# Weight sections prepared in an overlapped order in a two-layer hybrid attention and retention kernel

## The chip, the cores and the metric

The kernel runs on one core of a Trainium2 chip. The metric is the device time of one execution in microseconds (us), from the kernel's start to its end on that core; lower is better. Beside it stands one execution that was recorded by the hardware profiler, from which every row below comes.

## What is computed

The input is a sequence of 2048 tokens with 1024 features. Two layers follow each other, and each adds to the stream what a group of heads makes of it: eight heads of chunked softmax attention with a learned bias by distance (64 features each) and four heads of retention with rotary phases (128 features each), both gated. A last normalization ends it.

```python
def hybrid_layer(x, norm_gain, w_in, w_out, rel_bias, cos, sin):
    hn = rms_norm(x, norm_gain)
    proj = hn @ w_in
    aq, ak, av, ag, rq, rk, rv, rg = split(proj)          # 8 sections of 512 columns
    ya = chunked_rel_attention(aq, ak, av, rel_bias)      # own chunk of 64 and 8 before it
    yr = chunkwise_retention(rq, rk, rv, cos, sin)        # decay per head, RMS norm per head
    y = concatenate([ya * silu(ag), yr * silu(rg)])
    return x + y @ w_out
```

The time goes into the products with `w_in` (1024 x 4096) and `w_out` (1024 x 1024) of each layer, in near-fp32 accuracy.

## The kernel before

**Number format.** Each fp32 matrix is split into two f16 halves, hi and lo, and a product is three matmuls (hi·hi, hi·lo, lo·hi). For that, a section of weights is scaled first by a power of two that is found from its sum of squares. That is the preparation that the change touches.

**Tiling.** A layer runs over four head groups `s` (two attention heads and one retention head each), and each group over four token blocks `n` of 512 tokens. A group uses eight sections of 128 columns of `w_in`: four (`TSEC`, line 289) give q, k and the retention's q and k in transposed form, four (`VSEC`, line 290) the values and gates. For each (layer, s, n) the program runs `dense_T` (matmul in line 753), then `dense_V` (matmul in line 772). Each has 12 rounds of eight matmuls of 128x512, which are the bulk of TensorE's work.

**Rounds.** `run` (line 1174) goes over the rounds of a dense pass. In each round it starts what was deferred with `later`, makes one step of the attention of the block before (`attention`, line 798), and pulls steps of background work. An attention block has eight units (a, hx), three rounds each: scores `S` on TensorE, bias and maximum on VectorE (line 824), exponential and the hi copy on ScalarE (827, 829), the lo half on GpSimd (830), a transposing DMA `pT` on SyncE (832), and two units later the product `o` with the values on TensorE (840 to 842). The output is scaled on VectorE (846 to 852). Retention's steps (`r`, `sh`, `rss`, `yr`) lie between.

**Background work.** `push(gen, steps)` hands a generator over with a number of steps; a step runs until the generator's next `yield`. In each round, `run` pulls the steps that are still to do divided by a number of rounds that are left (`thirds`), rounded up. So the number of steps, the number of `yield`s in the generator and `thirds` decide in which round which instruction is written. Where `thirds` is larger than the number of rounds of a pass, the work runs on into the next pass.

**Order.** TensorE, VectorE, ScalarE and GpSimd run their instructions in the order in which the program writes them. SyncE, which issues the DMAs, is ordered by the scheduler from estimated times, apart from those that are put in turn by hand.

**Preparation of the next group's weights.** `prep_T` (line 385) prepares the four transposed sections and is pushed with 25 steps when block n = 1 starts (in the first group of layer 0: n = 3, with 18 thirds). `prep_V` (line 417) prepares the four others and is pushed with 23 steps before `dense_V` of block n = 3; it runs over that pass's 12 rounds and on into `dense_T` of the next group. One section passes through these steps:

- load: 512 KB into one of three buffers of the pool `w4` (line 297)
- square: ScalarE squares the section and adds up (312), VectorE rounds the sum to bf16 (319, `mb`)
- scale: TensorE adds over the partitions by a one-column matmul with ones (326, `ms`) into one of four small PSUM buffers that attention uses too; VectorE makes a power of two of it (328 and 143 to 147)
- split: ScalarE writes the hi half (333), one step later VectorE the lo half (336)
- units: after certain sections a few small products of scales (`T_units`, `V_units`, lines 344 and 400)

In `prep_V` the last two sections share one scale: line 456 adds the two sums, and one scale follows. The path for layer 1's first group (`halves`, `prep_V_next`) and the preparation of `w_out` (`prep_O`, `prep_Omax`) are of their own.

There are six preparations by `prep_T` and six by `prep_V`, three in each layer.

Of the kernel before, what the change touches and what calls it, by code (L numbers as in the profile page):

```python
# [13 lines left out]
ALU = mybir.AluOpType  # L14
# [13 lines left out]
def hybrid_trunk(ctx: ExitStack, tc: tile.TileContext, x, pos, gain, gcol, w_in, w_out, rel, fgain,  # L28
# [8 lines left out]
    act, dve, pool, pe, sp = nc.scalar, nc.vector, nc.gpsimd, nc.tensor, nc.sync  # L37
# [100 lines left out]
    def norm_scale(sq, nm, ig=None, k=14):  # L138

        e = b2.tile([P, 1], I32, tag="p2e", name=f"e{nm}")  # L140
        s = b2.tile([P, 1], I32, tag="p2s", name=f"s{nm}", bufs=8)
        i = b2.tile([P, 1], I32, tag="p2i", name=f"i{nm}", bufs=12)
        dve.tensor_scalar(e, sq.bitcast(I32), 24, 23, op0=ALU.logical_shift_right, op1=ALU.logical_shift_left)
        dve.tensor_scalar(s, e, -1.0, float((190 + k) << 23), op0=ALU.mult, op1=ALU.add)
        dve.tensor_scalar(i, e, float((64 - k) << 23), None, op0=ALU.add)
        if ig is not None:
            dve.tensor_tensor(i.bitcast(F32), i.bitcast(F32), ig, op=ALU.mult)
        return s.bitcast(F32), i.bitcast(F32)

    gains = {}  # L150
# [166 lines left out]
    def lowp(m1, nm):  # L317
        mb = b2.tile([P, 1], BF16, tag="mb", name=f"mb{nm}", bufs=4)
        dve.tensor_copy(mb, m1)
        return mb  # L320

    def allsum(mb, nm, lo=2.0 ** -60, ps=None):

        if ps is None:
            ps = psR.tile([P, 512], F32, tag="small", name=f"ms{nm}")
        pe.matmul(ps[:, 0:1], ones.to_broadcast([P, P]), mb, start=True, stop=True)
        m2 = b2.tile([P, 1], F32, tag="m2", name=f"m2{nm}")
        dve.tensor_scalar(m2, ps[:, 0:1], lo, None, op0=ALU.max)
        return m2
# [54 lines left out]

    def prep_T(l, s, g, halves=False, w=None):
        w = w or Sections(l, s, g, halves)
        w.load(0)
        yield
        for j in range(4):
            if j < 3:  # L390
                w.load(j + 1)
            yield
            w.square(j)
            yield
            yield
            yield
            w.scale(j)
            yield from w.split(j)
# [18 lines left out]
    def prep_V(l, s, g):  # L417
        nm = f"V{l}_{s}"
        g.vh = b3.tile([P, KT, 512], F16, tag="wh", name=f"wh{nm}")
        g.vl = b3.tile([P, KT, 512], F16, tag="wl", name=f"wl{nm}")  # L420
        c0 = s * P
        sts = []

        def ld(j):
            o = VSEC[j] * 512 + c0
            sts.append(load_sec(w_in[l, :, o:o + P], f"{nm}{j}"))

        def sq(j):
            return sumsq(sts[j], f"{nm}{j}", g.vh[:, :, j * P:(j + 1) * P])

        def cv(j, s_):
            return convert(sts[j], g.vh[:, :, j * P:(j + 1) * P], g.vl[:, :, j * P:(j + 1) * P], s_)

        def rest(k):
            for _ in range(k):
                yield

        ld(0)
        ld(1)
        yield  # L440
        iv = [None] * 3
        m1 = [None] * 2
        for j in range(2):
            yield
            m1[j] = lowp(sq(j), f"{nm}{j}")
            yield from rest(3)
            m = allsum(m1[j], f"{nm}{j}")
            sv, iv[j] = norm_scale(m, f"{nm}{j}", gains[l].i)
            yield from cv(j, sv)
            ld(2 + j)  # L450
        yield from rest(1)
        m2 = sq(2)
        yield
        yield from rest(1)
        m3 = sq(3)
        dve.tensor_tensor(m2, m2, m3, op=ALU.add)
        m2 = lowp(m2, f"{nm}2")
        yield
        yield from rest(2)
        m = allsum(m2, f"{nm}2")  # L460
        sv, iv[2] = norm_scale(m, f"{nm}2", gains[l].i)
        for _ in V_units(l, s, g, iv, nm):
            pass
        yield from cv(2, sv)
        yield from cv(3, sv)
        g.vdone = 4
# [683 lines left out]
    def push(gen, steps):  # L1150
        bg.append([gen, steps])
# [17 lines left out]
    def grp(l, s):  # L1169
        if (l, s) not in groups:  # L1170
            groups[l, s] = Grp()
        return groups[l, s]
# [220 lines left out]
    for l in range(DEPTH):  # L1393
        gO = [Grp(), Grp()]
        go = Grp()
        for s in range(NSW):
            g = grp(l, s)
            for n in range(NS):
                first = (l, s, n) == (0, 0, 0)
                if not first:  # L1400
                    st = St()
                    states[l, s, n] = st
                    dT = dense_T(l, s, n, g, st)
                else:
                    st = st0
                if n == 0 and not first:
                    bs, bt = bias_scratch(l, s), bias_tiles(l, s, g)
                    later(3, lambda bs=bs: next(bs))
                    for k in (7, 11, 17, 21):
                        later(k, lambda bt=bt: next(bt))  # L1410
                if (l, s) == (0, 0) and 0 < n < NS - 1:
                    if n == 1:
                        push(t1, TAB_STEPS - 7)
                    pairs = [xs0[0], w4.tile([P, D], F32, tag="w4", name="rows8") if n == 1 else xs0[1]]
                    pairs = [(w_[:, 0:D], w_[:, D:2 * D]) for w_ in (r_.bitcast(F16) for r_ in pairs)]
                    push(norms_from_input(range(4 * n + 4, 4 * n + 8), late[0:4] if n == 1 else None, pairs,
                                          tables(n + 1, [xs0[n + 1][:, i * 256:(i + 1) * 256] for i in range(4)])), 21)
                if (l, s, n) == (0, 1, 1):
                    for l_ in range(1, DEPTH):
                        gr = gain_scale(l_)  # L1420
                        later(2, lambda gr=gr: next(gr))
                        later(10, lambda gr=gr: next(gr))
                        later(18, lambda gr=gr: next(gr))
                if n == (NS - 1 if (l, s) == (0, 0) else 1):
                    if s + 1 < NSW:
                        push(prep_T(l, s + 1, grp(l, s + 1)), 25)
                    else:
                        push(prep_O(l, 0, gO[0], go), 9)
                if n == NS - 1 and s == 1 and l + 1 < DEPTH:
                    gain_load(l + 1)  # L1430
                if n == 2 and s == 2:
                    push(prep_Omax(l, go), 21)
                last = n == NS - 1 and s == NSW - 1
                if last:
                    us = []
                    push(wout_first(l, go, us), 9)
                if not first:
                    run(dT, att, 12 if last else 10 if n == 0 else 18 if (l, s, n) == (0, 0, NS - 1) else 22 if (l, s) == (0, 0) else 24)
                if n == NS - 1:
                    if s + 1 < NSW:  # L1440
                        push(prep_V(l, s + 1, grp(l, s + 1)), 23)
                    else:
                        push(with_turn(prep_O(l, 1, gO[1], go), us), 12)
                run(dense_V(l, s, n, g, st), att, 24 if n == NS - 1 and s < NSW - 1 else 12)
                if first:
                    sp_order.__exit__(None, None, None)
                    ring["free"] = True
                if att[0] is not None:
                    drain(att[0])
                att = [attention(l, s, n, g, st, states.get((l, s, n - 1)))]  # L1450
        pull(1000)
        if l + 1 == DEPTH:
            ring["fg"] = b3.tile([P, D], F32, tag="wh", name="fg")
            sp.dma_start(ring["fg"], fgain.to_broadcast([P, D]))
        wT = Sections(l + 1, 0, grp(l + 1, 0), True) if l + 1 < DEPTH else None
        wo = wout(l, go, gO, us, wT)

        def rounds_of(k):
            run((next(wo) for _ in range(k)), att, k)

        rounds_of(30)
        if l + 1 < DEPTH:
            push(prep_T(l + 1, 0, grp(l + 1, 0), True, wT), 21)
            rounds_of(36)
            pull(1000)
            pV = prep_V_next(l + 1, grp(l + 1, 0))
            next(pV)
            rounds_of(18)
            next(pV)
            rounds_of(6 * NT - 90)  # L1470
            push(pV, 13)
        else:
            rounds_of(6 * NT - 36)
        run(wo, att, 15)
# [60 lines left out]
```

## Time and profile before

| | us |
| --- | --- |
| runs of the kernel | 2062.57, 2067.20, 2067.78 |
| median | 2067.2 |
| the profiled execution | 2061.84 |
| its span, from the first to the last instruction | 2060.0 |

| engine | short name in rows | busy |
| --- | --- | --- |
| TensorE | PE | 97% |
| TensorE's weight loads | PEld | 51% |
| VectorE | DVE | 60% |
| ScalarE | ACT | 55% |
| GpSimd | POOL | 33% |

The granted TensorE clock is 0.996 of full speed over the span.

How to read rows: a timeline row has the start in us from the span's start, the duration, engine, line and operation, what is written and from which tiles it is read (with shape and type), and in brackets the idle time of the engine before it and what ended it. A row of waits has the instruction that waited, what it waited for, then the total in us, the number of times and the longest. A row of windows has the stretch, its length, the busy time of PE, PEld, DVE, ACT and POOL with the number of instructions, the granted clock, the share of the DMA engines and GB/s. SPq is SyncE's DMA queue. Matmuls are pipelined, so a matmul's duration is longer than the distance between two starts, and that distance is the pace.

### The profile page before, as it was taken

What the parts mean: (1) busy time and instruction counts of PE and PEld (TensorE: products, weight loads), DVE (VectorE), ACT (ScalarE), POOL (GpSimd) and SP (SyncE); (2) the same over time, 40 slices, a digit from 0 to 9 for tenths busy, and PEclk for the clock granted to TensorE, in tenths of its full rate; (3) what the DMA queues carried; (4) which work ended last, traced back from release to release, by engine and by line L of the source; (5) the groups of instructions that cost most, each with busy time, mean ns of one, the idle gap of its engine ahead of it and who ended that gap; (6) DMA issues with size and microseconds to landing.
All of it is one profiled execution on the core that took longest, in us unless ns stands there. A gap on an engine that the chain in (4) does not pass through costs nothing. (4 is left out here: it accounts for less than half of the span.)

```text
span 2060.0 us, 39310 instructions
## 1 busy us (share of the span) xinstructions
PE 1997.9 (97%) x14014; PEld 1049.6 (51%) x14014; DVE 1231.2 (60%) x3817; ACT 1137.7 (55%) x2530; POOL 687.9 (33%) x701
## 2 busy tenths in 40 slices
PE   6988999999999999999999999999999999999998
PEld 4444555555555555554444555555555555555443
DVE  6776656556556655666653556555655565567643
ACT  6566665556565654655443546554656565455432
POOL 0244343444344433430003343433344334333100
PEclk9999999999999999999999999999999999999999
DMA  8778664547584764799865546554756775658964
GB/s 230 169 156 177 156 146 112 112 111 166 113 187 111 166 135 101 164 206 262 233 174 120 126 103 149 120 127 103 155 115 145 163 151 126 131 116 188 228 203 135
DMA packets 645700, 313.62 MB, mean 152 GB/s; under 512 B 459232, under 2 KB 602080, under 8 KB 645504
## 3 DMA queue, kind: packets, MB, share of 16 engines
q1 hardware_dynamic: 645504, 311.12, 66.1%
q8 instruction: 109, 1.79, 0.4%
q14 instruction: 87, 0.71, 0.1%
HBM read 123.26 MB, written 41.98 MB: 80 GB/s over the span
## 5 line engine op out<-in xcount | busy, mean ns | idle before, releaser
L830 POOL TENSOR_TENSOR pq<-sc,pq 128x640 f16<-128x640 f32 (+4 forms) x256 | 319.7, 1249 | 861.0 <-ACT pq L829 451.5
L827 ACT ACTIVATE sc<-sc,mq,cT 128x640 f32<-128x640 f32 (+4 forms) x256 | 218.4, 853 | 615.7 <-DVE rl L846 298.3
L772 PE MATMUL dV<-whV,hTh 128*128 128x512 f16 x1024 | 353.3, 381 | 6.9 <-DVE gt L790 6.4
L772 PE MATMUL dV<-whV,hTl 128*128 128x512 f16 x1024 | 352.5, 380 | 0.0
L772 PE MATMUL dV<-wlV,hTh 128*128 128x512 f16 x1024 | 352.5, 380 | 0.0
L753 PE MATMUL dT<-hTh,whT 128*128 128x512 f16 x1008 | 347.0, 379 | 1.3 <-DMA hTh<-xa 1.1
L753 PE MATMUL dT<-hTl,whT 128*128 128x512 f16 x1008 | 347.1, 379 | 0.0
L753 PE MATMUL dT<-hTh,wlT 128*128 128x512 f16 x1008 | 347.1, 379 | 0.0
L772 PEld LDWEIGHTS <-hTh 128*128 128x128 f16 x2048 | 196.5, 98 | 224.0 <-DVE gt L790 9.0
L753 PEld LDWEIGHTS <-whT 128*128 128x128 f16 x2016 | 192.3, 98 | 210.6 <-issue 4.5
L824 DVE CUSTOM_DVE_ANT_0 sc<-S,bias 128x640 f32<-128x640 f32 (+4 forms) x256 | 188.1, 735 | 86.2 <-PE S L821 84.6
L1127 PE MATMUL dO<-whO,yly 128*128 128x512 f16 x512 | 194.7, 380 | 1.4 <-DMA yly<-hTl 1.4
L1127 PE MATMUL dO<-wlO,yhy 128*128 128x512 f16 x512 | 194.8, 380 | 0.0
L1127 PE MATMUL dO<-whO,yhy 128*128 128x512 f16 x512 | 194.7, 380 | 0.0
L829 ACT ACTIVATE pq<-sc 128x640 f16<-128x640 f32 (+4 forms) x256 | 171.5, 670 | 8.1
L1127 PEld LDWEIGHTS <-yhy 128*128 128x128 f16 x1024 | 100.0, 98 | 115.1 <-issue 1.4
L772 PEld LDWEIGHTS <-hTl 128*128 128x128 f16 x1024 | 99.2, 98 | 110.8 <-issue 1.9
L753 PEld LDWEIGHTS <-wlT 128*128 128x128 f16 x1008 | 97.3, 98 | 111.5 <-issue 4.0
L820 PE MATMUL S<-k,q 128*128 128x128 f16 (+3 forms) x592 | 142.0, 266 | 0.0
L840 PE MATMUL o<-v,pT 128*128 128x65 f16 x1120 | 129.4, 193 | 6.0 <-DMA pT<-pq 6.0
L841 PE MATMUL o<-v,pT 128*128 128x64 f16 x1120 | 129.8, 195 | 0.0
L821 PE MATMUL S<-k,q 128*128 128x128 f16 (+3 forms) x592 | 129.3, 266 | 0.0
(352 smaller groups left out, 3464.1 us busy)
## 6 DMA issues: line engine op xcount, KB each, us to landing
q<-qq SPq DMA_DIRECT2D x128, 128.0 KB, 2.4
yyy<-y_d SPq DMA_DIRECT2D x32, 512.0 KB, 4.6
stT<-in_w_in_dram SPq DMA_DIRECT2D x27, 512.0 KB, 4.9
stV<-in_w_in_dram SPq DMA_DIRECT2D x26, 512.0 KB, 4.8
k<-kk SPq DMA_DIRECT2D x128, 64.0 KB, 2.0
swp<-rot SPq DMA_DIRECT2D x64, 128.0 KB, 3.0
tabc<-tab SPq DMA_DIRECT2D x32, 256.0 KB, 2.9
tabs<-tab SPq DMA_DIRECT2D x32, 256.0 KB, 3.1
```

Source lines behind the costliest of these rows:

```text
L753: pe.matmul(ps, w_[:, j, kt, :], h_[:, kt, :], start=(m == 0), stop=(m == 23))
L772: pe.matmul(ps, h_[:, kt, a * P:(a + 1) * P], w_[:, kt, :], start=(m == 0), stop=(m == 23))
L820: pe.matmul(o, st.q[:, hx, 0, cs], k_, start=True, stop=False)
L821: pe.matmul(o, st.q[:, hx, 1, cs], k_, start=False, stop=True)
L824: dve.tensor_tensor_reduce(out=v, in0=S[:, 0:w], in1=g.bias[hx][:, 640 - w:640], scale=1.0, scalar=-3.0e38, op0=ALU.add, op1=ALU.max, accu ...
L827: act.activation(v, v, AF.Exp, bias=m[:, 0:1], scale=g.c[:, 0:1])
L829: act.activation(pq[:, 0:w], v, AF.Copy)
L830: pool.tensor_tensor(pq[:, w:2 * w], v, pq[:, 0:w], op=ALU.subtract)
L840: pe.matmul(o[:, 0:65], u.p[:, b, :], v_[:, 0:65], start=(b == 0), stop=False)
L841: pe.matmul(o[:, 0:64], u.p[:, b, :], v_[:, 65:129], start=False, stop=False)
L1127: pe.matmul(ps, h_[:, kt, :], w_[:, kt, :], start=(m == 0), stop=(m == 23))
```

## The change

In both generators the order of sections is changed from one after the other to an overlapped one: sections 0 and 1 are loaded in the first step; the square of a section is written, then one step later the scale and the split of the section before it; sections 2 and 3 are loaded after the squares 0 and 2. `prep_T` ends with one more step and the scale and split of section 3; `prep_V` with two steps, the joint scale of sections 2 and 3, the units and both splits. The number of yields falls, and with it the steps pushed: 25 to 19 for `prep_T`, 23 to 20 for `prep_V`. The instructions themselves are the same in kind and number on every engine. The path with `halves` keeps the old order.

```diff
@@ -384,6 +384,23 @@
 
     def prep_T(l, s, g, halves=False, w=None):
         w = w or Sections(l, s, g, halves)
+        if not halves:
+            w.load(0)
+            w.load(1)
+            for j in range(4):
+                for _ in range((2, 2, 0, 1)[j]):
+                    yield
+                w.square(j)
+                if j in (0, 2):
+                    w.load((j + 4) // 2)
+                yield
+                if j:
+                    w.scale(j - 1)
+                    yield from w.split(j - 1)
+            yield
+            w.scale(3)
+            yield from w.split(3)
+            return
         w.load(0)
         yield
         for j in range(4):
@@ -431,34 +448,32 @@
         def cv(j, s_):
             return convert(sts[j], g.vh[:, :, j * P:(j + 1) * P], g.vl[:, :, j * P:(j + 1) * P], s_)
 
-        def rest(k):
-            for _ in range(k):
-                yield
+        def scale(j):
+            sv, iv[j] = norm_scale(allsum(m[j], f"{nm}{j}"), f"{nm}{j}", gains[l].i)
+            return sv
 
         ld(0)
         ld(1)
-        yield
-        iv = [None] * 3
-        m1 = [None] * 2
-        for j in range(2):
-            yield
-            m1[j] = lowp(sq(j), f"{nm}{j}")
-            yield from rest(3)
-            m = allsum(m1[j], f"{nm}{j}")
-            sv, iv[j] = norm_scale(m, f"{nm}{j}", gains[l].i)
-            yield from cv(j, sv)
-            ld(2 + j)
-        yield from rest(1)
-        m2 = sq(2)
-        yield
-        yield from rest(1)
-        m3 = sq(3)
-        dve.tensor_tensor(m2, m2, m3, op=ALU.add)
-        m2 = lowp(m2, f"{nm}2")
-        yield
-        yield from rest(2)
-        m = allsum(m2, f"{nm}2")
-        sv, iv[2] = norm_scale(m, f"{nm}2", gains[l].i)
+        iv, m = [None] * 3, [None] * 3
+        for j in range(4):
+            for _ in range((2, 2, 0, 1)[j]):
+                yield
+            m1 = sq(j)
+            if j < 2:
+                m[j] = lowp(m1, f"{nm}{j}")
+            elif j == 2:
+                m2 = m1
+            else:
+                dve.tensor_tensor(m2, m2, m1, op=ALU.add)
+                m[2] = lowp(m2, f"{nm}2")
+            if j in (0, 2):
+                ld((j + 4) // 2)
+            yield
+            if 0 < j < 3:
+                yield from cv(j - 1, scale(j - 1))
+        yield
+        yield
+        sv = scale(2)
         for _ in V_units(l, s, g, iv, nm):
             pass
         yield from cv(2, sv)
@@ -1423,7 +1438,7 @@
                         later(18, lambda gr=gr: next(gr))
                 if n == (NS - 1 if (l, s) == (0, 0) else 1):
                     if s + 1 < NSW:
-                        push(prep_T(l, s + 1, grp(l, s + 1)), 25)
+                        push(prep_T(l, s + 1, grp(l, s + 1)), 19)
                     else:
                         push(prep_O(l, 0, gO[0], go), 9)
                 if n == NS - 1 and s == 1 and l + 1 < DEPTH:
@@ -1438,7 +1453,7 @@
                     run(dT, att, 12 if last else 10 if n == 0 else 18 if (l, s, n) == (0, 0, NS - 1) else 22 if (l, s) == (0, 0) else 24)
                 if n == NS - 1:
                     if s + 1 < NSW:
-                        push(prep_V(l, s + 1, grp(l, s + 1)), 23)
+                        push(prep_V(l, s + 1, grp(l, s + 1)), 20)
                     else:
                         push(with_turn(prep_O(l, 1, gO[1], go), us), 12)
                 run(dense_V(l, s, n, g, st), att, 24 if n == NS - 1 and s < NSW - 1 else 12)
```

Written out by rounds of the token block's 24, with the first push (layer 0, n = 3) apart, steady state: before, the T squares are written at rounds 2, 8, 14, 20 and their scales at 5, 11, 17, 23; after, the squares at 3, 6, 9, 13 and the scales at 7, 10, 14, 17. For V (V0 to V11 are the rounds of `dense_V` of block 3, d0 on those of the next group's `dense_T`), the last square moves from d4 to d1, the joint scale with the units from d7 to d4, and the last lo half from d10 to d7.

## The prediction

> **What bounds the kernel now.** I read the page first, then the windows by stage, then what PE waits for, and last the timelines round one preparation of the second kind.
>
> ```profile
> span 2060.0 us, 39310 instructions
> PE 1997.9 (97%) x14014; PEld 1049.6 (51%) x14014; DVE 1231.2 (60%) x3817; ACT 1137.7 (55%) x2530; POOL 687.9 (33%) x701
> ...
> 195.00:290.00 95.00, 89.07 (x690) 48.10 (x691) 54.42 (x198) 61.11 (x136) 34.73 (x33) 1.00 0.70 161
> 290.00:860.00 570.00, 568.48 (x4232) 304.44 (x4231) 337.64 (x1150) 325.06 (x765) 223.10 (x222) 1.00 0.60 132
> ...
> 1070.00:1860.00 790.00, 787.54 (x5731) 417.80 (x5730) 452.69 (x1509) 441.83 (x1043) 301.98 (x301) 1.00 0.59 130
> ```
>
> PE is the bound: 97% of the span, and 568.48 of 570 us and 787.54 of 790 us in the two long windows (PE is the first busy time of a row, DVE the third, ACT the fourth). Those windows hold five of the six preparations; there the change has 570 − 568.48 + 790 − 787.54 = 4.0 us of idle PE to take away, whatever waits it removes on other engines. What idle time it could remove lies in the first preparation, 195 to 290 us, with 95 − 89.07 = 5.9 us. The waits of PE in that window:
>
> ```profile
> PE msT L326 <- DVE mbT L319: 2.3, 3, 1.3
> PE msV L326 <- DVE ya L852: 2.1, 2, 1.5
> PE msV L326 <- DVE mbV L319: 1.3, 1, 1.3
> PE dT L753 <- DMA hTh<-xa: 1.1, 1, 1.1
> ...
> 230.47 0.16 PE L326 MATMUL msT<-mbT,ones 128*128 128x1 bf16 x1 [0.56 <-DVE mbT L319]
> ```
>
> Six waits (3 + 2 + 1) at the one-column matmul that sums the squares over the partitions: 2.3 + 2.1 + 1.3 = 5.7 us. These are the waits that a longer distance between square and scale can remove.
>
> **The pace of PE.** Matmuls of 512 columns, after a long wait and after a shorter one:
>
> ```profile
> 931.96 0.20 PE L840 MATMUL o<-v,pT 128*128 128x65 f16 x1 [2.45 <-DMA pT<-pq]
> ...
> 934.26 0.63 PE L1127 MATMUL dO<-wlO,yhy 128*128 128x512 f16 x1
> 934.69 0.63 PE L1127 MATMUL dO<-whO,yly 128*128 128x512 f16 x1
> ...
> 270.03 0.16 PE L326 MATMUL msV<-mbV,ones 128*128 128x1 bf16 x1 [1.51 <-DVE ya L852]
> 270.05 0.38 PE L753 MATMUL dT<-hTl,whT 128*128 128x512 f16 x1
> 270.27 0.38 PE L753 MATMUL dT<-hTh,whT 128*128 128x512 f16 x1
> ```
>
> They start 0.216 us apart at full pace (270.05 to 270.27), so a round of eight takes 1.7 us. After a wait of 2.45 us they start 0.43 us apart, for eight of them: 8 × (0.43 − 0.216) = 1.7 us more. After one of 1.51 us nothing is added. So a new stall below 1.5 us costs its own length, and one above 2.45 us 1.7 more. The Trainium skill ("TensorE: Matmul & The Clock Gate", Part 1: The HAM clock gate) says that the half rate comes after an idle window of about 3.4 us. By that rule stalls of 2.4 us in the slower rival below would cost nothing beside their length; the row of 2.45 us here disagrees, and the row decides.
>
> **The loads.** Two at once changes next to nothing: the buffers' loads land in 4.9 us, and few instructions wait for them.
>
> ```profile
>   DVE mbT L319: 43.1, 23
> ...
>   ACT whT L312: 1.2, 1
> DMA to landing us min/median/max: 3.2/4.9/7.5
> ...
> 452.04 0.38 SPq L297 DMA_DIRECT2D stV<-in_w_in_dram  x1
> ```
>
> That is the view of the transposed sections' load buffer: what waited for its readers (a scale on PE or DVE's rounding, 43.1 us of idle engines off the path), one square of 1.2 us, and the landing times; the last row is a load of SP's timeline, whose section is squared at 471.33 (below), 19 us later. In the built program, SP's queue takes the first three loads of a group as their buffers come free already before the change; only the fourth moves, by one transposed attention block. I cost it at 0; cover is the time that a section lies in its buffer before its square. Without that cover a square would be up to 1.2 us late, the one wait of the view.
>
> **First preparation (fourth token block of the first group), −3.0 us.** Counted in rounds by the step budget, the four T scales stand 1, 1, 3 and 2 rounds behind their squares before (two steps a round), and 4, 4, 5 and 2 after (one step a round at the end of the pass, another square between); the first V scale 3 before and 4 after. The longest of these waits is 1.3 us, under the 1.7 of one round, so two of the msT waits go and the one on `mbV`; the third msT wait is the fourth scale's, at 230.47, and with 2 rounds it keeps its 0.56. The two waits on `ya` are for an older attention unit's result, which must leave a PSUM buffer first; the scales that have them stand three rounds behind their squares before and after, so I leave them standing. (2.3 − 0.6) + 1.3 = 3.0 us. Bounds: −5.7 (all six) and 0 (each is replaced by the next item in DVE's order).
>
> **T preparations of the other five groups: 0.** Nineteen steps instead of 25 over the same 24 rounds: the squares come up to seven rounds earlier, the finished weights four, and each scale stands four rounds behind its square instead of three. They run under attention that is short (second token block); the windows above show PE with 0.3% idle there. If cover failed, the price is one lo half on DVE, 1.28 us (the row at 481.90 below), per section.
>
> **V preparations: the new cost.** They run from the V pass of a group's last token block through ten rounds of the next group's first pass, beside long attention. Twenty steps in place of 23 bring the last square, the joint scale with the units of V, and the last two halves three rounds (one attention unit, 475.24 − 468.55 = 6.7 us with its waits) forward. The order on DVE and ACT is the program's, so this block goes in front of another unit. One of the six windows, before, on DVE and then ACT:
>
> ```profile
> 468.55 0.82 DVE L824 CUSTOM_DVE_ANT_0 sc<-S,bias 128x640 f32<-128x640 f32 x1 [0.31 <-PE S L821]
> ...
> 472.49 0.47 DVE L456 TENSOR_TENSOR m1V<-m1V,m1V 128x1 f32<-128x1 f32 x1 [2.85 <-ACT whV L312]
> ...
> 475.24 0.82 DVE L824 CUSTOM_DVE_ANT_0 sc<-S,bias 128x640 f32<-128x640 f32 x1 [0.71 <-PE S L821]
> ...
> 476.24 0.15 DVE L328 TENSOR_SCALAR m2V<-msV 128x1 f32<-128x1 f32 x1
> ...
> 479.91 0.16 DVE L410 TENSOR_TENSOR gqkV<-gqkV 128x1 f32<-128x1 f32 x1 [2.89 <-ACT reV L407]
> ...
> 481.90 1.28 DVE L336 SCALAR_TENSOR_TENSOR wlV<-stV,sV,whV 128x1024 f16<-128x1024 f32 x1 [0.21 <-ACT whV L333]
> ...
> 484.70 0.82 DVE L824 CUSTOM_DVE_ANT_0 sc<-S,bias 128x640 f32<-128x640 f32 x1
> ```
> ```profile
> 471.33 1.04 ACT L312 ACTIVATE whV<-stV 128x1024 f16<-128x1024 f32 x1
> ...
> 476.42 0.92 ACT L827 ACTIVATE sc<-sc,mq,cT 128x640 f32<-128x640 f32 x1 [3.28 <-DVE m2V L328]
> 477.37 0.74 ACT L829 ACTIVATE pq<-sc 128x640 f16<-128x640 f32 x1
> 478.01 0.19 ACT L193 ACTIVATE urvV<-dcs 128x1 f32<-128x1 f32 x1
> ...
> 479.58 0.29 ACT L407 ACTIVATE reV<-reV,gqkV 128x1 f32<-128x1 f32 x1
> ...
> 480.74 1.13 ACT L333 ACTIVATE whV<-stV,sV 128x1024 f16<-128x1024 f32 x1
> ```
>
> Here `sc` at 468.55 is the second unit (0,1) of attention, 475.24 the third (1,0), 484.70 the fourth (1,1). Between the third and the fourth stands the block from `m2V` at 476.24 to the first lo half, which ends at 481.90 + 1.28 = 483.18: 6.9 us, in which DVE waits 2.89 for ACT's unit operations, which wait for the third unit's exponential and copy. The third unit has only the last square ahead of it and a gap of 2.85.
>
> After, that block stands between 468.55 and 475.24. Its start is the end of the second unit's `sc` and `mq`, about 1.1 us after 468.55, and the second unit itself comes about 1.5 us late, because DVE now waits for the last square (1.04 us on ACT) ahead of it: 471.1. The row distances of the block then give: scale till 471.9; ACT's exponential and copy 1.7, so units on ACT from 472.8 to 474.7 (478.01 to 479.87 before); DVE's six small operations and the older unit's output to 476.2; hi half 1.13 beside them to 476.7, lo half to 478.0; rope's `kk` and retention's state, which stand there anyway, about 1 us; `sc` at 479.0. That is 479.0 − 475.24 = 3.7 us late. The lower bound takes the block as 6.9 less the 0.9 us of attention's own work in it, less the two gaps of 2.85 and 0.71 that it fills: 2.4 us. I take 3.5, near the step by step value, which follows the order.
>
> Who waits for it: ACT's exponential, POOL's lo, SP's transpose, then PE.
>
> ```profile
> 478.24 1.39 POOL L830 TENSOR_TENSOR pq<-sc,pq 128x640 f16<-128x640 f32 x1 [5.29 <-issue]
> ...
> 478.54 0.58 SPq L637 DMA_DIRECT2D tabc<-tab  x1
> ...
> 480.19 1.78 SPq L832 DMA_TRANSPOSE pT<-pq  x1
> ...
> 485.00 2.38 SPq L297 DMA_DIRECT2D stT<-in_w_in_dram  x2
> ...
> DMA to landing us min/median/max: 4.0/5.6/5.6
> ...
> 487.11 0.19 PE L840 MATMUL o<-v,pT 128*128 128x65 f16 x1
> ...
> PE o L840 <- DMA pT<-pq: 0.3, 1, 0.3
> ```
>
> Before: issued at 480.19, landed 4.0 to 5.6 us later (the three transposes of this stretch), at 484.2 to 485.8; PE takes it at 487.11. In hand: 1.3 to 2.9 us. The issue stood 0.56 us behind POOL's end (478.24 + 1.39 = 479.63) in SP's queue, behind table and bias loads; a later transpose need not. So it is 3.5 − 0.5 = 3.0 late at the queue, and PE waits between 3.0 − 2.9 = 0.1 and 3.0 − 1.3 = 1.7 us. On SP one load of 512 KB (one of the two at 485.00) moves ahead of the third unit's transpose in the built program; it takes DMA time there, which speaks for the upper half. I take 0.9 a window, six windows: +5.4 us; bounds 0 and, with the full 3.7 and a backlog at 5.6 us, 2.4 each, +14.4. The fourth unit, the late one today (PE waits 0.3 us for its transpose in the window 1470 to 1500 us, the last row), is relieved in return; little is to be had there.
>
> **The sum.** 2061.8 (profiled execution: span 2060.0 and 1.8 around it) − 3.0 + 0 + 5.4 = 2064.2. The median of the runs shown, 2067.2, lies 5.4 above that execution; so 2069.6, against 2067.2.
>
> **Rivals.** Faster: in the V windows landings are at the quick end (4.0 us), so slack holds, and all six waits of the first preparation go; 5.7 us less, and the fourth unit's relief is worth up to 0.3 in each of six windows, 1.8: 2067.2 − 7.5 = 2059.7. For it: DVE is 60% busy and has time to catch up. Against it: DVE's in-order waits, not its load, make the delay.
>
> Slower: the moved block makes PE wait for the third unit's transpose by the upper bound, 2.4 us in each of six windows, and each then pays 1.7 at the lower clock: 6 × 4.1 − 3.0 = 21.6, 2088.8; without the clock 6 × 2.4 − 3.0 = 11.4, 2078.6, which I give as this rival's time. It decides from a stall of (6.2 + 3.0) / 6 = 1.5 us a window on. For it: four of the values in the chain are estimates from in-order rows that tend to add up, and the load moved ahead. Against it: in the trace PE hardly waits for transposes in these windows.
>
> The change doesn't do what it says: preparation is hidden but for the first one, whose waits turn into waits for the next item on DVE: 2067.2.
>
> **How the numbers follow.** Forecast (about even, 2069.6) 0.38; no effect at all 0.06; faster 0.21; slower 0.35. A change of under 0.3%, 6.2 us, can't be told from none here. Faster by more than that: 0.20, the rival but for its weaker cases. Slower by more: 0.37, the slower rival and the upper edge of the forecast. Within: 0.43. Low end of the range 2059, the faster rival's time with 0.7 us to spare; high end 2084, between the slower rival without and with the clock. The forecast's own range is 2063 to 2075.
>
> **What would show it.** In the first preparation: PE idle of 195 to 290 us falls from 5.9 to about 3, and the list of waits there loses two of msT and the `mbV` one. In the V windows: the `m2V` block stands between the second and third `sc`, the third `sc` starts some 3.5 us later against PE's matmuls, and the line of PE's `o` waiting for pT gains up to six entries of about 0.9. If those entries are missing, the slack is larger than I read; if they exceed 2 us with matmuls 0.43 apart behind them, the slower rival holds. It would be wrong at the root if the T windows, costed at 0, showed waits of PE at dense matmuls for `wlT`, or if the long windows together gained more than the 4.0 us that they have to give.

## The result

| | median us | runs |
| --- | --- | --- |
| before | 2064.0 | 10, from 2061.5 to 2067.8 |
| after | 2070.1 | 10, from 2067.1 to 2074.0 |

The ratio is 1.0027, with an interval of 1.0018 to 1.0036: the change costs 6.0 us by the medians, and between 3.7 and 7.4 by the interval. That it costs something is clear of the noise. The predicted 2069.6 lies 0.5 us off, but that is partly luck: the forecast was a move of +2.4 from the 2067.2 of three runs, and ten runs put the start at 2064.0. A start that was 3.2 too high and a move that was 3.6 too small nearly cancel. What has to be explained is +6.0 where +2.4 was worked out.

The page of the changed kernel, and then the windows that the prediction used (length, then busy time of PE, PEld, DVE, ACT and POOL, the granted clock, the share of the DMA engines, GB/s):

```profile
span 2068.9 us, 39344 instructions
PE 1999.9 (97%) x14014; PEld 1048.5 (51%) x14014; DVE 1226.2 (59%) x3817; ACT 1138.4 (55%) x2530; POOL 684.2 (33%) x701
```
```profile
195.00:290.00 95.00, 89.20 (x692) 47.71 (x691) 59.47 (x208) 61.24 (x139) 36.01 (x34) 1.00 0.75 164
290.00:860.00 570.00, 565.14 (x4195) 301.78 (x4194) 333.60 (x1138) 321.65 (x756) 220.72 (x219) 1.00 0.58 130
...
1070.00:1860.00 790.00, 783.14 (x5683) 414.82 (x5682) 442.22 (x1499) 437.96 (x1032) 294.55 (x296) 1.00 0.58 129
```

In the first preparation PE is idle for 95 − 89.2 = 5.8 us, as before (5.9). In the two long windows its idle time grew from 1.5 to 4.9 and from 2.5 to 6.9, together by 7.7 us. So the gain did not come, and the cost is in the two long windows, which hold the five preparations in steady state. What PE waited for in the three windows, in this order, of the changed kernel (total, times, longest):

```profile
PE o L855 <- DMA pT<-pq: 3.5, 3, 1.7
PE r L889 <- DVE dT L897: 1.5, 2, 1.4
PE o L855 <- DVE ya L867: 0.8, 1, 0.8
...
PE o L855 <- DMA pT<-pq: 2.9, 2, 2.0
...
PE o L855 <- DMA pT<-pq: 4.7, 3, 2.2
```

The first three rows are the first preparation. All six waits at `ms` are gone from it (5.7 us before), and 3.5 + 1.5 + 0.8 = 5.8 us of other waits stand in their place. The other two rows are the five V windows (the stretches of the V preparations) that lie in the long windows: one wait each, for the third unit's transpose, 7.6 us in all, where before there was one of 0.3, for a fourth unit's.

The V window that the prediction followed, on DVE after the change:

```profile
466.15 0.47 DVE L467 TENSOR_TENSOR m1V<-m1V,m1V 128x1 f32<-128x1 f32 x1 [2.85 <-ACT whV L312]
...
469.11 0.82 DVE L839 CUSTOM_DVE_ANT_0 sc<-S,bias 128x640 f32<-128x640 f32 x1
...
470.10 0.15 DVE L328 TENSOR_SCALAR m2V<-msV 128x1 f32<-128x1 f32 x1
...
473.77 0.16 DVE L427 TENSOR_TENSOR gqkV<-gqkV 128x1 f32<-128x1 f32 x1 [2.89 <-ACT reV L424]
...
475.76 1.28 DVE L336 SCALAR_TENSOR_TENSOR wlV<-stV,sV,whV 128x1024 f16<-128x1024 f32 x1 [0.42 <-ACT whV L333]
...
477.76 0.82 DVE L839 CUSTOM_DVE_ANT_0 sc<-S,bias 128x640 f32<-128x640 f32 x1
...
483.61 0.82 DVE L839 CUSTOM_DVE_ANT_0 sc<-S,bias 128x640 f32<-128x640 f32 x1
```

The second unit's `sc` at 469.11, then the block from `m2V` to the lo half, then the third unit's `sc` at 477.76. SP's queue, the landing time of the one transpose issued at 482.18, and PE:

```profile
478.19 0.38 SPq L297 DMA_DIRECT2D stT<-in_w_in_dram  x1
...
481.05 0.43 SPq L600 DMA_DIRECT2D bias<-toep  x1
482.18 2.25 SPq L847 DMA_TRANSPOSE pT<-pq  x1
```
```profile
DMA to landing us min/median/max: 6.3/6.3/6.3
```
```profile
488.50 0.20 PE L855 MATMUL o<-v,pT 128*128 128x65 f16 x1 [1.96 <-DMA pT<-pq]
...
489.68 1.03 PE L787 MATMUL dV<-whV,hTl 128*128 128x512 f16 x4
```

The transpose lands at 482.18 + 6.3 = 488.48, and PE starts at 488.50, 1.96 us after it was free. Before, the same transpose had a landing time of its own of 5.6 us:

```profile
DMA to landing us min/median/max: 5.6/5.6/5.6
```

Two things are later, then: the issue, and the landing after it. Counted back from when PE was ready (487.11 before, 488.50 − 1.96 = 486.54 after), `sc` starts 11.87 us ahead before and 8.78 after, 3.1 later; the issue 6.92 ahead before and 4.36 after, 2.6 later; the landing takes 0.7 more. 2.6 + 0.7 less the slack of 1.3 (487.11 − 485.8) is the wait of 2.0. Ahead of the transpose stands, 4 us earlier, a load of 512 KB that before stood behind it.

### The profile page after: what moved, and what is told of

Its sections match the earlier page's. It is cut to its first block, busy times and chain, and to the rows that moved or that the text cites. A ratio compares the mean times of both kernels' runs of the same rounds, so it can differ in the third digit from the quotient of the medians.

```text
span 2068.9 us, 39344 instructions
## 1 busy us (share of the span) xinstructions
PE 1999.9 (97%) x14014; PEld 1048.5 (51%) x14014; DVE 1226.2 (59%) x3817; ACT 1138.4 (55%) x2530; POOL 684.2 (33%) x701
## 5 line engine op out<-in xcount | busy, mean ns | idle before, releaser
L855 PEld LDWEIGHTS <-pT 128*128 128x128 f16 x1120 | 105.5, 97 | 55.5 <-DMA pT<-pq 25.4
```

What stands on the lines that cost most here:

```text
L855: pe.matmul(o[:, 0:65], u.p[:, b, :], v_[:, 0:65], start=(b == 0), stop=False)
```

## The experiments

Theories on record: *block* (VectorE's order makes the third unit late), *load* (the 512 KB ahead of the transpose do), *T* (the denser work on the transposed sections), *square* (the last square ahead of the second unit), and, from the second set on, *two-part* (block and load are each within the slack, their sum is not).

| run | median us | ratio to before, interval |
| --- | --- | --- |
| T sections alone | 2061.1 | 0.9990 (0.998 to 1.000) |
| V sections alone | 2070.5 | 1.0034 (1.0022 to 1.0046) |
| block three steps later | 2067.8 | 1.0028 (1.0018 to 1.0037) |
| T loads held | 2062.0 | 0.9994 (0.9985 to 1.0003) |
| T and w_out loads held | 2061.2 | 0.9986 (0.9976 to 0.9996) |
| before, loads held | 2061.1 | 0.9987 (0.9978 to 0.9995) |
| T sections alone, loads held | 2061.8 | 0.9988 (0.9979 to 0.9996) |
| block one step later | 2070.4 | 1.0030 (1.0019 to 1.0041) |
| before, loads held, copy added | 2062.2 | 0.9999 (0.9991 to 1.0008) |
| after, loads held, copy added | 2070.9 | 1.0045 (1.0030 to 1.0060) |
| block three steps later, loads held | 2066.4 | 1.0021 (1.0012 to 1.0030) |

The ratios are to runs of the kernel before that were taken beside each set; their medians are 2062.3 (the first four runs of the table), 2063.7 (the next four) and 2062.8 (the last three).

### One generator at a time

The new `prep_T` with the old `prep_V` and 23 steps for it, and the other way round with 25 steps for `prep_T`. One line of the first, against the changed kernel:

```diff
...
-                        push(prep_V(l, s + 1, grp(l, s + 1)), 20)
+                        push(prep_V(l, s + 1, grp(l, s + 1)), 23)
...
```

> The new order for the transposed sections alone (19 steps); the V sections as before (23 steps). Block theory (the cost of the change is the V block of joint scale, units and lo half in front of the third attention unit): no wait of PE for pT at the third unit in the windows after 290 us, and two of the three msT waits of the first preparation gone; 1 to 5 us less than before. T theory (the denser T squares and splits cost): half or more of the 6 us of the change, so 3 us or more above before.

> The new order for the V sections alone (20 steps); the transposed sections as before (25 steps). Block theory: the five waits of the later windows for the third unit's pT stay as in the changed kernel (1.0 to 2.3 us each, 8 to 10 us in all with the slow matmuls behind one of them), so 6 to 11 us above before. T theory: within 2 us of before.

Measured: T alone 1.3 us less with an interval that touches no change, V alone 8 us more than before's 2062.3 (7.0 by the ratio). The whole cost is in the V sections. T alone, waits of PE in the first preparation:

```profile
PE msV L326 <- DVE ya L869: 3.4, 3, 1.5
PE dT L770 <- DMA hTh<-xa: 1.0, 1, 1.0
PE o L857 <- DVE ya L869: 0.8, 1, 0.8
PE r L891 <- DVE dT L899: 0.4, 1, 0.4
```

The three waits of `msT` on `mbT` are gone, as expected or better; but the three V scales wait for `ya` now, 3.4 us where `ya` and `mbV` had 2.1 + 1.3 = 3.4 before, and `o` waits for `ya` too. So the gain of that part is about 1 us (5.7 against 3.4 + 0.8 + 0.4). V alone, the third unit's waits in the two long windows:

```profile
PE o L838 <- DMA pT<-pq: 4.0, 2, 2.0
...
PE o L838 <- DMA pT<-pq: 2.5, 3, 1.7
```

Five waits of 6.5 us: those of the changed kernel, without anything of T. The load is ahead of the third unit's transpose here too, by 4.2 us:

```profile
484.03 0.53 SPq L297 DMA_DIRECT2D stT<-in_w_in_dram  x1
...
488.27 2.10 SPq L830 DMA_TRANSPOSE pT<-pq  x1
```

With T alone it stands behind that transpose, as before (two loads at 485.68, the transpose at 480.77). So the load moves with the V sections, though it belongs to the transposed ones.

### The block back in its old place

```diff
+        yield
+        yield
+        yield
         yield
         yield
         sv = scale(2)
```

> The changed kernel with three more steps ahead of the joint scale of the V sections, and nothing else: scale, units and splits of the last two sections fall where they fell before, the last square stays where the change puts it. Block theory: the waits for the third unit's pT go, the gain of the first preparation stays; 2 to 6 us less than before, 8 to 12 less than the changed kernel. Square theory (the last square ahead of the second unit is what makes attention late): the waits stay, 6 us above before.

In the order of the program, DVE's work round the third unit is that of the kernel before, and SP takes the load after the transpose again. The waits at the third unit are gone; the one wait for pT that is left in the long windows, 1.1 us at 703.8, is the fourth unit's. Yet the time hardly falls: 1.0028. Neither theory had both. The first preparation shows a new wait:

```profile
PE dV L790 <- ACT whV L333: 2.4, 1, 2.4
PE o L858 <- DMA pT<-pq: 2.1, 1, 2.1
```

There the first dense V tile of the next group comes before the last hi half of its weights. In the first preparation the change had moved the block by two rounds only, so by the built order three more steps put that half one round later than before. On ACT it now stands behind the exponential of the fourth unit (275.83) and behind a step on the `bias` table that waits 1.97 us for GpSimd:

```profile
279.49 0.83 ACT L609 ACTIVATE bias<-bias,ciT 128x640 f32<-128x640 f32 x1 [1.97 <-POOL bias L608]
...
280.42 1.13 ACT L333 ACTIVATE whV<-stV,sV 128x1024 f16<-128x1024 f32 x1
```

The square theory falls by the waits: the last square stood ahead of the second unit, and the third unit's waits were gone. It falls by the time as well in a run further down, where the square and the block both stay in the changed place and the loads are held (0.9986). The profiled execution here (2064.8 us) was 2.9 us faster than the median of its runs; what the others lose beyond it stays open.

With one more step in place of three:

> The changed kernel with one more step ahead of the joint scale of the V sections (three more took the waits of the later windows away). The block then stands behind the older unit's output but still ahead of the third unit, with the first lo half; by the built order the load stands right ahead of the third unit's transpose and not in front of the table loads. Two-part theory: the block is shorter by part of its wait for ScalarE, the load still ahead: waits of 0.5 to 2 us at the third unit stay in most windows; 3 to 8 us above before. If only the load's place in front of the table loads mattered, the waits would go and the time lie within 2 us of before.

The waits stay, 3.7 us in three waits in the first long window and 2.2 in three in the second (one of the six, 0.4 us, is a fourth unit's), and each V window has a new one of 1.0 us besides (`r` for `dT`, which stands behind the block on DVE). It came out as the two-part theory had it.

### The load out of the way

The load of section 1 is queued on SyncE behind the latest transpose that the program has written; DVE's order is that of the changed kernel. The load that follows it in the queue moves along: in the window followed, loads stand at 478.19 and 486.38 in the changed kernel and at 515.11 and 515.73 here.

```diff
-            sp.dma_start(st, v)
+            if held and "pt" in ring:
+                with tc.issue_after(ring["pt"].ins):
+                    sp.dma_start(st, v)
...
-            later(1, lambda: sp.dma_start_transpose(out=u.p, in_=pq[:, 0:2 * w]))
+            later(1, lambda: ring.update(pt=sp.dma_start_transpose(out=u.p, in_=pq[:, 0:2 * w])))
```

> The changed kernel, in which the load of section 1 of the next group's transposed weights is queued behind the latest attention transpose that the program has written, so it no longer runs ahead of the third unit's transpose; the V block stays where the change puts it. Block theory: the third unit's transpose is issued as late as in the changed kernel, and lands at most 1 us earlier; the waits shrink to 0.3 to 1.5 us each, 1 to 5 us above before. Load theory (the 512 KB ahead of the transpose make it late): the waits go, 3 us less than before.

Measured 0.9994: the whole cost of the change is gone, with the V block where the change puts it. The block theory alone falls. The load theory's 3 us less than before is at the edge of the interval (1.2 less by the ratio, at most 3.1). The transpose of the same window, its landing time, and the waits in the two long windows:

```profile
483.76 1.57 SPq L851 DMA_TRANSPOSE pT<-pq  x1
```
```profile
DMA to landing us min/median/max: 3.7/3.7/3.7
```
```profile
PE o L859 <- DMA pT<-pq: 0.6, 1, 0.6
...
PE o L859 <- DMA pT<-pq: 0.9, 1, 0.9
```

It lands in 3.7 us instead of 6.3. The two waits that are left, at 696 and 1699 us, are in the windows of the last group, where the load that runs ahead is one of `w_out`, which was not held. That is a control inside one run: same block, same place, load held or not. Holding that one as well, and then the same hold in the kernel before and with T alone:

> As the run with held loads, and the second load of w_out's weights is held too, which takes the place of the transposed weights' load in the third group's windows. In the run before, those two windows alone kept a wait of PE at the third unit (0.8 and 1.1 us), the transpose landing 4.9 and 5.3 us after its issue against 3.1 to 3.7 in the other windows. Two-part theory (the V block makes the transpose about 3 us later, the load ahead of it lengthens its landing by some 2 us; only the sum is more than the slack): no wait at the third unit is left; 1 to 4 us less than before. Block theory: the two waits stay, the landings don't change.

> The kernel before with the same two loads held, nothing else. It tells whether holding the loads saves time by itself. Two-part theory: the third unit's transpose has slack there anyway, so within 2 us of before; the fourth unit's transposes, which PE waits for by a few tenths, land up to 1 us earlier. If holding were a gain of its own, 4 us or more less than before, and the held run with the change would say nothing of the block.

> The new order for the transposed sections alone, the V sections as before, and both loads held. Two-part theory: like the run with the transposed sections alone, 0 to 4 us less than before; the waits of 0.2, 0.8 and 0.6 us for pT that it showed after 1690 us go. A candidate for the best version.

All three come to 0.9986 to 0.9988 of before. In the run with the change and both loads held, the waits for pT in the long windows are down to this one:

```profile
PE o L859 <- DMA pT<-pq: 0.2, 1, 0.2
```

So holding is worth some 2.7 us by itself (1.0 to 4.5 by the interval), a little more than the 2 us that were expected at most. Where that gain lies is open. The fourth unit's transpose in the window followed landed in 4.0 us before and in 3.0 with the loads held, but PE did not wait for it in either, the long windows of the kernel before have only 0.3 us of waits for pT, and the two profiled executions differ by 0.3 us (2061.84 and 2061.50). With the loads held the change is worth nothing either way. By the ratios each of the three beats the kernel before by 2 to 3 us, and the changed kernel, which was not run beside them, by 8 to 9.

### The load put back, as another transfer

A copy of 512 KB from DRAM to DRAM between the copies of k, in the six windows, with the real loads held; nothing reads it. It is additional work on the DMA engines.

```diff
-                    sp.dma_start(st.k[64:128, 1, :], kh[64:128, :])
+                    i = sp.dma_start(st.k[64:128, 1, :], kh[64:128, :])
+                    if n == 0 and s > 0:
+                        with tc.issue_after(i.ins):
+                            sp.dma_start(dp.tile([P, KT, P], F32, tag=f"cp{l}_{s}", name=f"cp{l}_{s}"),
+                                         w_in[l, :, 0:P].rearrange("(k p) c -> p k c", p=P))
```

> The kernel before with both loads held (which ran at 0.9987 of before), and in each of the six windows one copy of 512 KB of weights from DRAM to DRAM added between the copies of k, where the changed kernel has its load; nothing reads the copy. It is the load without the moved V block. Two-part theory: the third unit's transpose lands up to 2 us later against a slack of 1.2 to 1.9 us; waits of 0 to 0.8 us a window, so 0 to 5 us above the run with held loads. Load theory (the load alone makes the change's cost): waits of 1 to 2 us in each window, 6 to 12 us above it.

> The changed kernel with both loads held (which ran at 0.9986 of before), and the same copy of 512 KB added at the same place: the moved V block and a load ahead of the third unit's transpose again, but not the same load. Two-part theory: the waits of 1 to 2.3 us a window come back; 6 to 13 us above the held run, and clearly more than what the copy costs without the block. If holding helped in another way than by clearing the way for the transpose, little comes back.

| ratio to before | no copy | copy of 512 KB ahead of the transpose |
| --- | --- | --- |
| V block in the old place | 0.9987 | 0.9999 |
| V block in the new place | 0.9986 | 1.0045 |

This is the test that settles it. The block without a transfer costs nothing; the transfer without the block costs 0.0012, some 2.5 us, which is within the noise (the intervals of 0.9987 and 0.9999 overlap); both together cost 0.0059, some 12 us (by the medians: 2070.9 − 2062.76 × 0.9986 = 11.0). The copy is work that the change does not add, so 12 us is not the price of the change; that the two cost together what neither costs alone is what carries over. Landing time of the third unit's transpose in the window followed, for block and copy:

```profile
DMA to landing us min/median/max: 5.9/5.9/5.9
```

against this for block without copy:

```profile
DMA to landing us min/median/max: 4.0/4.0/4.0
```

The waits for pT with block and copy in the long windows:

```profile
PE o L863 <- DMA pT<-pq: 2.2, 2, 1.6
...
PE o L863 <- DMA pT<-pq: 1.7, 2, 1.3
```

These are from the fastest execution of that kernel (2065.6 us), so they are less than what its median has. With the copy but without the block the waits are small:

```profile
PE o L848 <- DMA pT<-pq: 0.6, 2, 0.4
```

The landing times of the third unit's transpose in all six V windows, from the same four profiles, say how the two work together:

| landing, us | no copy | copy of 512 KB ahead |
| --- | --- | --- |
| V block in the old place | 5.2 to 5.5 | 5.2, 5.3 and 6.1 to 7.4 |
| V block in the new place | 3.1 to 4.6 | 4.5 to 6.2 |

In the changed kernel it is 5.2 to 6.5. In the old place the transpose is issued at most 0.4 us behind the bias load and lands slowly, but it has the slack. In the new place it is issued 1.0 to 1.8 us behind the bias load (0.5 to 1.0 with the copy), lands faster, and so makes up for part of its lateness; with a transfer of 512 KB some 4 us ahead it loses most of that again. That the distance from the table and bias loads makes it faster is the likely reason; it was not tried by itself.

### Three steps later, with the loads held

> The run with the joint scale three steps later, with both loads held. Without holding it stayed 0.28% above before although its waits at the third unit were gone, which neither theory had expected; its profile shows 2.5 us at the first dense V tile behind the first preparation (the hi half of V came too late), and the fourth unit's transposes with no slack. Two-part theory: the first stays (2 to 5 us with the slow matmuls), the second goes: 0 to 5 us above before, and below the run without holding.

Measured 1.0021, inside what was expected. The wait of the first dense V tile is larger here, and longer than expected:

```profile
PE dV L794 <- ACT whV L337: 4.9, 1, 4.9
```

The eight matmuls behind it take 3.57 us where others take 1.89, 1.7 more. Together that is 6.6 of the 7.0 us by which this run lies above the kernel before with the same hold (1.0021 against 0.9987). So moving the block back is a cure of the steady windows that the first preparation pays for; moving the load is one for which these runs show no price.

## Why the prediction was right, and where it was not

**The bound, and where a gain could be:** right. PE has the same busy time to 2 us (1999.9 against 1997.9), and the long windows gave nothing away.

**The loads at 0:** wrong, and the step that failed. It asked only whether a section comes in time for its square, and it does. The price is at somebody else: a load that moves up in the queue lies ahead of a transpose on the DMA engines. The prediction named the moved load in the V part and let it speak for the upper half of a range; it should have had a term of its own, one that counts only together with the block. Taking the load away brought the changed kernel from 1.0027 to 0.9986, 8.5 us, and the kernel before only from 1 to 0.9987, 2.7 us: some 6 us, the whole cost of the change, hang on the two together.

**First preparation, −3.0:** too much. All six waits at `ms` went, more than was forecast, but 5.8 us of other waits stand in their place. Part of them is the price of the V part in its sixth window: 1.19 us at 280.11 and 0.52 at 287.17, for the transposes of the third and the fourth unit. With both loads held these two are gone, and the waits of the first preparation are:

```profile
PE r L893 <- DVE dT L901: 1.8, 3, 1.3
PE dT L772 <- DMA hTh<-xa: 1.1, 1, 1.1
PE o L859 <- DMA pT<-pq: 1.1, 1, 1.1
PE o L859 <- DVE ya L871: 0.8, 1, 0.8
```

The wait on `hTh` was there before. PE is idle for 95 − 90.67 = 4.3 us then, against 5.9 before (5.8 with the same hold), so some 1.5 us are left of the 3.0: the item behind took most of each wait's place, near the bound of 0 that the text named. With T alone about 1 us was left. There the waits on `ya`, which the prediction left standing, grew from 2.1 to 3.4 us.

**T windows at 0:** right. T alone shows no wait for `wlT` or `mbT` in the long windows.

**V windows, +5.4:** right in place, too small, and the mechanism was half of it. The block stands between the second and third unit, `sc` is 3.1 us late (3.5 was used), the transpose's issue 2.6 (3.0 was used). The wait per window is 7.6 / 5 = 1.5 us, not 0.9. The sum worked it out from the block's lateness, with the load only as a reason for the upper half, and the block alone costs nothing (0.9986 against 0.9987). The mis-sized term is the landing: the sum took 4.0 to 5.6 us as if that were scatter. It is not. In the window followed, the transpose takes 5.6 right behind the table and bias loads; 3.7 to 4.0 when it comes later and the loads are held, which pays for most of the lateness; and 6.3 with a load of 512 KB ahead.

**The clock:** the matmuls were slow behind one of the five waits. The rows of the changed kernel:

```profile
1289.43 0.20 PE L855 MATMUL o<-v,pT 128*128 128x65 f16 x1 [2.16 <-DMA pT<-pq]
...
1290.92 3.26 PE L787 MATMUL dV<-whV,hTl 128*128 128x512 f16 x8
```

Eight matmuls take 3.26 us there, so some 0.41 from start to start if the last takes 0.38, after a wait of 2.16; after the one of 1.96 at 488.50 four take 1.03, full pace. That looks like an edge near 2 us, but it is none. In the same trace a longer wait is followed by matmuls 0.22 us apart:

```profile
933.78 0.20 PE L855 MATMUL o<-v,pT 128*128 128x65 f16 x1 [2.30 <-DMA pT<-pq]
...
934.25 0.38 PE L1142 MATMUL dO<-whO,yly 128*128 128x512 f16 x1
934.47 0.38 PE L1142 MATMUL dO<-whO,yhy 128*128 128x512 f16 x1
```

And one and the same wait, 2.54 us for a scale near 42 us, is followed by full pace in the kernel before (at 43.58) and by eight matmuls 0.43 us apart in the kernel before with the loads held (from 42.64 on, the wait ends at 41.33). So the length of a wait does not decide by itself in these traces, and the prediction's bracket of 1.51 to 2.45 us was no rule either; what else decides was not looked into. The Trainium skill ("TensorE: Matmul & The Clock Gate", Part 1: The HAM clock gate) gives an idle window of about 3.4 us. Read as the length of one wait, that does not agree with this trace, where 2.16 us was enough.

**The rivals:** the slower one named the right place, and decides from 1.5 us a window on; the measured 1.5 lies just there, and 6.0 us is just under the 6.2 that it was set against. But its 2.4 us a window was too much, and 2070.1 is far nearer to the forecast than to its 2078.6. The faster one and the one without effect are out: the first preparation gave next to nothing, as the latter had it, but the V windows cost 7.6 us of waits, and the interval excludes no change. It also shows that the 0.3% below which the prediction could not tell a change from none was too coarse for ten runs of each kernel.

## What to carry to other kernels

When a background load moves up in a queue, price it at the transfers that it now precedes, not at its own reader: here a transpose landed in 4.0 us without a transfer of 512 KB some 4 us ahead of it and in 5.9 with one. A path with slack can take one delay and not two, so each delay should be tried with and without the other before one of them is called harmless. And a wait that is taken away in front of an in-order engine is a gain only up to the wait behind it: of 5.7 us some 1.5 were left here.

## What was not expected of the hardware

The transpose of one attention unit takes 3.1 to 7.4 us from issue to landing in the profiles of the table of landings above. The late issue went with a faster landing: in the window followed it came 2.4 us later at the queue, counted back from when PE was ready, and took 4.0 us in flight instead of 5.3 (both with the loads held). So a block of VectorE's work that delays it costs nothing as long as no large transfer stands ahead of it (0.9986 with the block, 0.9987 without). And the same wait of PE, 2.54 us, is followed by matmuls at half pace in one execution and at full pace in another.
